# First layer's entry of a hybrid SSD/MLA decoder step: order of squares, weight casts, convolutions and first loads

## Chip, cores and metric

The kernel runs on one core of a Trainium2 chip. The metric is device time in microseconds for one execution; lower is better. The core has a tensor engine (PE, with PEld for its weight loads), a vector engine (DVE), a scalar engine (ACT), GpSimd (POOL) and SyncE (SP, whose queue issues nearly all DMA transfers here).

## The reference

The reference is one inference step of a two-layer decoder in float32: a Mamba-2 SSD layer, then a multi-head latent attention layer, each with an RMSNorm ahead of it and a residual around it. There are 1024 prompt tokens and 8 x 8 sample tokens, 1088 rows of width 1024. Only the first layer's entry matters here:

```python
ln = rms_norm(h, norm_w[0])                       # per token, over 1024
proj = einsum('btd,de->bte', ln, w_in)            # z (2048), xBC (4096), dt (32)
xbc, new_buf = causal_conv(xbc, conv_buf, conv_w, conv_b)   # 4 taps along tokens
xbc = silu(xbc)
dt = softplus(dt_raw + dt_bias);  a_head = -exp(a_log)
y, new_state = ssd_scan(xs, dt, a_head, bm, cm, state)
```

## The kernel before

The whole program is written with a tile framework. The Python code traces instructions in program order; a scheduler with a timeline of its own then lays the order of each engine's queue, and each engine works its queue in that order. A few stages late in the program are ordered by hand; the entry is not.

**Token groups and rows.** The 1088 tokens are cut into three groups `TG` of 384, 384 and 320 columns, and each group into row tiles of 128 tokens (`TILES`, the last of 64). `norm_rows(gi)` loads a group's row tiles `xt` through SP, squares each on ACT with a sum (`sq`, an `ACTIVATE` and a read of the accumulator), takes the reciprocal roots `rs` (a DVE step and a power on POOL, in `rstd_of`), and scales the rows on DVE. There are `XB = 6` row buffers, so the third group's loads wait until the first group's rows have been transposed.

**Columns.** `norm_cols(gi)` turns the scaled rows into columns: for each of the eight blocks `d` of 128 features PE transposes the group's row tiles into one PSUM tile `xtp` (two buffers), ACT writes the rounded high part `xh` with the norm weight as scale (a "single column" below: one `d` of one group), and DVE writes the remainder `xl`. Every float32 product is three products of rounded parts: `xh` by weight high, `xl` by weight high, `xh` by weight low.

**Weights.** `load_w` issues a DMA of raw weights (`wraw`) on SP, splits them into a high part `wih` by a cast on ACT and a low part `wil` by a subtraction on DVE, or on POOL for the third and fourth block of group 0. Each block's weights come in two parts; there are two raw buffers (`RB`) and five pairs of split ones (`WB`).

**Blocks.** `Group` is one of eight SSD head groups. Its four blocks of 128 projected features (B, C and two of x) are projected for the three token groups (`proj_piece`, PSUM tile `pj`, two buffers), copied by ACT into `raw` (two buffers, so the third block needs the first one's), and convolved: ACT makes the first tap into `acc`, and three DVE steps `scalar_tensor_tensor` add the others. For group 0 the first two blocks run interleaved with the norm, token group by token group (`pair(0, both=True)`), and the rest follows after the norm. A SiLU on ACT over both blocks of a pair ends it. `gates` then projects z and, for group 0, dt, with weights split on POOL in `load_zdt` in two halves (`zdh`, `zdl`).

**Order of the entry.** `setup` loads the identity `ident`; `ssd_tiles` loads `alog` and takes its `Exp`; `norm_rows(0)` follows; `before()` loads the small vectors (norm weights, convolution weights) and the first two blocks' weights; `norm_cols(0)`, `norm_rows(1)`; `after()` loads constants and the convolution state; then the first projections, and so on by token group. `norm_rows(gi + 1)` is traced right after `norm_cols(gi)`.

Of the kernel before, what the change touches and what calls it, by code (L numbers as in the profile page):

```python
# [1 line left out]

# [1 line left out]

# [4 lines left out]
F32 = mybir.dt.float32  # L9
# [7 lines left out]
D = 1024  # L17
# [39 lines left out]
PAR = 0.62  # L57
WCOLS = (13, 15, 17, 19)
XDB = 2
YB = 2  # L60
SCAN = "csccsccsccscc"
XB = 6
# [69 lines left out]
def setup(k, stack):  # L132
    tc, nc, I = k.tc, k.nc, k.I
    cp = stack.enter_context(open_pool(tc, name="const", bufs=1))
    k.cp = cp
    k.ident = cp.tile([128, 128], F32, name="ident")
    nc.sync.dma_start(k.ident, I["c_ident"])
    k.nhalf = cp.tile([128, 36], F32, name="nhalf")
    nc.gpsimd.memset(k.nhalf, -0.5)
    k.dram = stack.enter_context(open_pool(tc, name="dram", bufs=1, space=DR))  # L140


def ssd_tiles(k):
    cp, nc = k.cs, k.nc
    k.masku = cp.tile([128, 128], F32, name="masku")
    k.masks = cp.tile([64, 128], F32, name="masks")
    k.negu = cp.tile([128, 128], F32, name="negu")
    k.negs = cp.tile([64, 128], F32, name="negs")
    k.blkm = cp.tile([64, NB], F32, name="blkm")
    k.yssq = cp.tile([128, 9, G], F32, name="yssq")  # L150
    k.tok = cp.tile([128, 9, 4, H], F32, name="tok")
    k.decp = cp.tile([128, H, 8], F32, name="decp")
    k.decs = cp.tile([128, 16, 8], F32, name="decs")
    k.dtb = cp.tile([128, H], F32, name="dtb")
    k.dsk = cp.tile([128, H], F32, name="dsk")
    k.tok3 = cp.tile([96, 2, H], F32, name="tok3")
    k.blk3 = cp.tile([96, 4], F32, name="blk3")
    k.alog = cp.tile([128, H], F32, name="alog")
    nc.sync.dma_start(k.alog, k.I["ssd_a_log"][0].partition_broadcast(128))
    nc.scalar.activation(k.alog, k.alog, AF.Exp)  # L160


def ssd_consts(k):
    nc, I = k.nc, k.I
    nc.sync.dma_start(k.masku, I["c_masku"])
    nc.sync.dma_start(k.masks, I["c_masks"])
    for neg, mask in ((k.negu, k.masku), (k.negs, k.masks)):
        nc.gpsimd.tensor_scalar(neg, mask, -NEG, NEG, op0=ALU.mult, op1=ALU.add)
    nc.sync.dma_start(k.blkm, I["c_blkm"])
    for j in range(3):  # L170
        nc.sync.dma_start(k.blk3[32 * j : 32 * j + 32], I["c_blkm"][:32, :4])
    nc.gpsimd.memset(k.yssq, 1.0)
    nc.sync.dma_start(k.dtb, I["ssd_dt_bias"][0].partition_broadcast(128))
    nc.sync.dma_start(k.dsk, I["ssd_d"][0].partition_broadcast(128))


def load_vectors(k, vp, psum):
    nc, I, cp = k.nc, k.I, k.cp
    if True:
        r1 = vp.tile([128, 128], F32, name="r1")  # L180
        nc.sync.dma_start(r1, I["ssd_conv_w"].rearrange("o k (b c) -> (o k b) c", c=128))
        r2 = vp.tile([68, 128], F32, name="r2")
        nc.sync.dma_start(r2[0:16], I["norm_w"].rearrange("l (b c) -> (l b) c", c=128))
        nc.sync.dma_start(r2[16:48], I["ssd_conv_b"].rearrange("o (b c) -> (o b) c", c=128))
        nc.sync.dma_start(r2[48:64], I["ssd_norm_w"].rearrange("o (b c) -> (o b) c", c=128))
        nc.sync.dma_start(r2[64:68], I["mla_q_norm_w"].rearrange("o (b c) -> (o b) c", c=128))
        k.vec = cp.tile([128, 196], F32, name="vec")
        p = psum.tile([128, 512], F32, tag="tr", name="vecp", bufs=PB["tr"])
        nc.tensor.transpose(p[:, :128], r1, k.ident)
        nc.tensor.transpose(p[:, 128:196], r2, k.ident[:68, :68])  # L190
        nc.vector.tensor_copy(k.vec, p[:, :196])
    k.convw = [k.vec[:, 32 * j : 32 * j + 32] for j in range(4)]
    k.normc = [k.vec[:, 128:136], k.vec[:, 136:144]]
    k.convb = k.vec[:, 144:176]
    k.ssdn = k.vec[:, 176:192]
    k.qn = k.vec[:, 192:196]


def rstd_of(k, out, ssq, n):
    nc = k.nc  # L200
    nc.vector.tensor_scalar(out, ssq, 1.0 / n, EPS, op0=ALU.mult, op1=ALU.add)
    m, n = out.shape[0], int(np.prod(out.shape[1:]))
    e = k.nhalf[:m, :n]
    if len(out.shape) == 3:
        e = e.rearrange("p (a b) -> p a b", a=out.shape[1])
    nc.gpsimd.tensor_tensor(out, out, e, op=ALU.pow)
# [9 lines left out]
def norm_rows(k, gi, load, pool, xbufs):  # L216
    nc = k.nc
    t0, n = TG[gi]
    idx = [i for i, (a, m) in enumerate(TILES) if t0 <= a < t0 + n]
    xs = []  # L220
    ssq = k.cp.tile([128, 3], F32, tag="nssq", name=f"ssq{gi}", bufs=2)
    nc.gpsimd.memset(ssq, 1.0)
    for j, i in enumerate(idx):
        m = TILES[i][1]
        xt = pool.tile([128, D], F32, tag="xt", name=f"xt{i}", bufs=xbufs)
        load(xt, i)
        sq = k.sqp(f"sq{i}")
        nc.scalar.activation(sq[:m], xt[:m], AF.Square, accum_out=ssq[:m, j : j + 1])
        xs.append((xt, m, TILES[i][0] - t0))
    rs = k.cp.tile([128, 3], F32, tag="nrs", name=f"rs{gi}", bufs=2)  # L230
    rstd_of(k, rs, ssq, D)
    for j, (xt, m, o) in enumerate(xs):
        nc.vector.tensor_scalar(xt[:m], xt[:m], rs[:m, j : j + 1], None, op0=ALU.mult)
    return xs


def norm_cols(k, gi, xs, wcol, hi, lo, psum):
    nc = k.nc
    t0, n = TG[gi]
    for d in range(8):  # L240
        p = psum.tile([128, 512], F32, tag="tr", name=f"xtp{gi}_{d}", bufs=PB["tr"])
        for xt, m, o in xs:
            nc.tensor.transpose(p[:, o : o + m], xt[:m, d * 128 : d * 128 + 128], k.ident[:m, :m])
        nc.scalar.activation(hi[:, d, t0 : t0 + n], p[:, :n], AF.Copy, scale=wcol[:, d : d + 1])  # L244
        nc.vector.scalar_tensor_tensor(
            lo[:, d, t0 : t0 + n], p[:, :n], wcol[:, d : d + 1], hi[:, d, t0 : t0 + n].bitcast(F32),
            op0=ALU.mult, op1=ALU.subtract)
    if gi == 2:
        nc.gpsimd.tensor_copy(hi[:, :, T:], lo[:, :, SEQ:].bitcast(F32))


def norm_steps(k, load, wcol, hi, lo, pool, psum, steps, xbufs, before=None, after=None, tail=False):
    if tail:
        for i in range(6, 9):
            k.hrows.append(scale_row(k, i, pool))
    rows = k.hrows[:3] if tail else norm_rows(k, 0, load, pool, xbufs)
    if before is not None:
        before()
        wcol = k.normc[0]
    for gi in range(3):  # L260
        norm_cols(k, gi, rows, wcol, hi, lo, psum)
        if gi < 2:
            rows = k.hrows[3 * gi + 3 : 3 * gi + 6] if tail else norm_rows(k, gi + 1, load, pool, xbufs)
        if after is not None and gi == 0:
            after()
        for st in steps:
            next(st)
# [55 lines left out]
def load_zdt(k, pool):  # L323
    nc = k.nc
    w = k.I["ssd_w_in"][0].rearrange("(k p) e -> p k e", p=128)
    k.wzd = []
    k.dtr = pool.tile([128, 9, H], F32, name="dtr")
    nc.gpsimd.memset(k.dtr[64:, 8], 0.0)
    for j in range(2):
        ks = slice(4 * j, 4 * j + 4)  # L330
        hi = pool.tile([128, 4, 288], F32R, name=f"zdh{j}")
        lo = pool.tile([128, 4, 288], F32R, name=f"zdl{j}")
        raw = load_raw(pool, 4, 288, 1)
        nc.sync.dma_start(raw[:, :, 0:256], w[:, ks, 0:256])
        nc.sync.dma_start(raw[:, :, 256:288], w[:, ks, DIN + CONV :])
        nc.gpsimd.tensor_copy(hi, raw)
        nc.gpsimd.tensor_tensor(lo, raw, hi.bitcast(F32), op=ALU.subtract)
        k.wzd += kslices((hi, lo), 4)


# [73 lines left out]
class Group:  # L414
    def __init__(self, k, g, pools):
        self.k, self.g = k, g
        self.wp, self.rp, self.gp, self.psum, ap = pools
        self.ap = ap[g % 2]
        self.raws = {}
        self.pre = {}  # L420
        self.xc = []
        self.ct = self.gp.tile([128, 4, 27], F32, tag="ct", name=f"ct{g}")
        self.z = None

    def pair(self, pi, both=False):
        k, g, nc = self.k, self.g, self.k.nc
# [23 lines left out]
    def block(self, bi, acc):  # L450
        k, g, nc, wp, rp, gp = self.k, self.g, self.k.nc, self.wp, self.rp, self.gp
        blk = (16 + g, 24 + g, 2 * g, 2 * g + 1)[bi]
        ws = self.pre.pop(bi, None) or self.weights(bi)
        raw = rp.tile([128, RAW], F32, tag="raw", name=f"raw{g}{bi}", bufs=2)
        smp = raw[:, 3 + SEQ :].rearrange("p (b w) -> p b w", w=NT + 3)
        nc.gpsimd.memset(raw[:, 0:3], 0.0)
# [16 lines left out]
        nc.scalar.activation(acc, raw[:, 3:], AF.Identity, bias=k.convb[:, blk : blk + 1],  # L473
                             scale=k.convw[3][:, blk : blk + 1])
        for j in range(3):
            nc.vector.scalar_tensor_tensor(acc, raw[:, j : j + n], k.convw[j][:, blk : blk + 1], acc,  # L476
                                           op0=ALU.mult, op1=ALU.add)

    def conv_out(self):
        k, g, nc, gp = self.k, self.g, self.k.nc, self.gp  # L480
# [1493 lines left out]
```

## Time and profile before

| | |
|---|---|
| median of 3 runs | 1986.58 us (1986.08, 1986.58, 1991.92) |
| profiled execution | 1992.53 us |
| its span, first to last instruction | 1990.7 us |
| PE busy | 1907.3 us (96% of the span) |
| DVE, ACT, POOL busy | 1200.6, 1110.7, 826.7 us |
| mean granted PE clock | 0.991 of full speed |
| DMA | 202.12 MB, mean 102 GB/s |

A row of the timeline gives start, duration, engine, source line, operation, out<-in by tile name, shape and count; in brackets stands the idle time of the engine before it and what ended it. `SPq` marks a DMA issue in SP's queue. Matmuls are pipelined, so the interval between two starts says more than a duration. Buffer numbers are left out of the names.

### The profile page before, as it was taken

Reading aid. Unit: us, or ns where it says so; the run is one execution under the profiler, and the core shown is the slowest. Engines: PE = TensorE matmul, PEld = TensorE weight load, DVE = VectorE, ACT = ScalarE, POOL = GpSimd, SP = SyncE. Lnnn points to the kernel's source line nnn. Section 1 sums busy time; section 2 is a strip of 40 time slices with the busy share of each in tenths; the row PEclk is TensorE's granted clock in tenths of the full one; section 3 lists DMA queues with packets and bytes.
Section 4 is the critical chain, followed back from the end, with each engine's and each line's share of the span. In section 5 each row is a group of like instructions: output and inputs, shape, how many; then the busy total and the mean of one; then the engine's idle time right before and its main releaser. Section 6 shows DMA issues by size and latency. Waiting matters only on the chain. (4 is left out here: it accounts for less than half of the span.)

```text
span 1990.7 us, 33385 instructions
## 1 busy us (share of the span) xinstructions
PE 1907.3 (96%) x12001; PEld 1735.5 (87%) x12001; DVE 1200.6 (60%) x2437; ACT 1110.7 (56%) x2535; POOL 826.7 (42%) x1010
## 2 busy tenths in 40 slices
PE   6999999999999999899999999999999999799998
PEld 5899999999999999788787998997888887688887
DVE  4537566656666656765533114566787786766665
ACT  5456767666666676732214224435777777745552
POOL 1327555555655555443003222204333434855541
PEclk9999999999999999999999999999999999999999
DMA  4213323333333332644534242222211213645451
GB/s 152 59 46 95 96 77 100 81 107 86 92 85 93 80 98 68 200 158 170 166 107 140 95 159 83 83 88 64 59 53 43 52 39 98 189 136 144 138 146 38
DMA packets 181228, 202.12 MB, mean 102 GB/s; under 512 B 18844, under 2 KB 147752, under 8 KB 180680
## 3 DMA queue, kind: packets, MB, share of 16 engines
q1 hardware_dynamic: 176008, 180.21, 30.5%
q0 software_dynamic: 4976, 19.66, 3.1%
q8 instruction: 95, 1.56, 0.3%
q14 instruction: 69, 0.57, 0.1%
q10 hardware_dynamic: 80, 0.13, 0.0%
HBM read 146.65 MB, written 53.28 MB: 100 GB/s over the span
## 5 line engine op out<-in xcount | busy, mean ns | idle before, releaser
L87 PE MATMUL pj<-xh,wih 128*128 128x384 f32 (+1 forms) x768 | 256.3, 338 | 9.2 <-ACT raw L460 4.5
L87 PE MATMUL pj<-xl,wih 128*128 128x384 f32 (+1 forms) x768 | 255.4, 333 | 0.0
L87 PE MATMUL pj<-xh,wil 128*128 128x384 f32 (+1 forms) x768 | 254.7, 332 | 0.0
L476 DVE SCALAR_TENSOR_TENSOR acc<-raw,vec,acc 128x1112 f32<-128x1112 f32 x96 | 141.6, 1478 | 25.6 <-ACT acc L473 24.7
L1332 POOL TENSOR_TENSOR tl<-P,th 128x384 fp32r<-128x384 f32 (+1 forms) x96 | 91.6, 955 | 155.6 <-ACT P L1330 113.8
L87 PEld LDWEIGHTS pj<-xh,wih 128*128 128x128 f32 x768 | 145.3, 190 | 11.5 <-ACT xh L244 5.2
L87 PEld LDWEIGHTS pj<-xl,wih 128*128 128x128 f32 x768 | 146.1, 190 | 0.9
L87 PEld LDWEIGHTS pj<-xh,wil 128*128 128x128 f32 x768 | 145.8, 190 | 0.4
L99 PE MATMUL pz<-wih,xh 128*128 128x256 f32 x504 | 142.8, 287 | 1.0 <-ACT z L516 1.0
L99 PE MATMUL pz<-wil,xh 128*128 128x256 f32 (+1 forms) x504 | 140.2, 284 | 0.0
L1329 ACT ACTIVATE th<-st 128x512 fp32r<-128x512 f32 x192 | 94.6, 492 | 70.6 <-PE st L1325 50.2
L579 ACT ACTIVATE M<-M,tok 128x128 f32<-128x128 f32 (+1 forms) x288 | 90.9, 386 | 70.9 <-DVE M L576 70.4
L99 PE MATMUL pz<-wih,xl 128*128 128x256 f32 x448 | 128.3, 286 | 0.0
L1621 POOL TENSOR_TENSOR kvl<-pgr,kvh 128x1024 fp32r<-128x1024 f32 x32 | 77.5, 2423 | 72.2 <-ACT kvh L1620 72.2
L99 PEld LDWEIGHTS pz<-wih,xh 128*128 128x128 f32 x504 | 95.9, 190 | 1.8 <-ACT z L516 1.5
L576 DVE TENSOR_TENSOR M<-M,negu 128x512 f32<-128x512 f32 x64 | 50.3, 786 | 73.2 <-DMA M<-acs_d 71.0
L1330 ACT ACTIVATE P<-st 128x512 f32<-128x512 f32 x192 | 93.5, 487 | 0.0
L99 PEld LDWEIGHTS pz<-wil,xh 128*128 128x128 f32 (+1 forms) x504 | 92.7, 184 | 0.7
L129 DVE TENSOR_TENSOR wil<-wraw,wih 128x512 fp32r<-128x512 f32 x88 | 72.2, 829 | 31.2 <-ACT wih L128 30.2
L1332 DVE TENSOR_TENSOR tl<-P,th 128x512 fp32r<-128x512 f32 x96 | 74.9, 780 | 21.4 <-ACT P L1330 20.9
L562 POOL TENSOR_TENSOR xdd<-xsT,tok 128x256 f32<-128x256 f32 x64 | 51.4, 803 | 81.9 <-ACT xsT L548 81.4
L99 PEld LDWEIGHTS pz<-wih,xl 128*128 128x128 f32 x448 | 85.3, 190 | 0.1
(827 smaller groups left out, 6318.4 us busy)
## 6 DMA issues: line engine op xcount, KB each, us to landing
wraw<-in_ssd_w_in SPq DMA_DIRECT2D x92, 256.0 KB
M<-acs_d SPq DMA_DIRECT2D x64, 256.0 KB
s<-in_state_ssm SPq DMA_DIRECT2D x32, 256.0 KB
y_d<-y SPq DMA_DIRECT2D x64, 128.0 KB
out_s_ssm<-s SPq DMA_DIRECT2D x32, 256.0 KB
wraw<-in_ssd_w_out SPq DMA_DIRECT2D x12, 512.0 KB
q_d<-qt SPq DMA_DIRECT2D x32, 192.0 KB
qp<-q_d SPq DMA_DIRECT2D x8, 768.0 KB
```

The costliest lines, as they stand in the source:

```text
L87: nc.tensor.matmul(out, a, b, start=(i == 0), stop=(i == n - 1))
L99: nc.tensor.matmul(o, a, b, start=(j == 0), stop=(j == len(ops) - 1))
L129: (eng or nc.vector).tensor_tensor(lo, src, hi.bitcast(F32), op=ALU.subtract)
L476: nc.vector.scalar_tensor_tensor(acc, raw[:, j : j + n], k.convw[j][:, blk : blk + 1], acc, op0=ALU.mult, op1=ALU.add)
L562: nc.gpsimd.tensor_tensor(v3(xdd), v3(xsT), hb(2), op=ALU.mult)
L576: nc.vector.tensor_tensor(M[:m, :, :m], M[:m, :, :m], (k.negs if smp else k.negu)[:m, :m].unsqueeze(1).to_broadcast([m, 4, m]), op=ALU.add)
L579: nc.scalar.activation(M[:m, h, :m], M[:m, h, :m], AF.Exp, bias=tk[:, 0, 4 * g + h : 4 * g + h + 1])
L1329: nc.scalar.activation(th[:, :n], ps[:, :n], AF.Exp, scale=SCALE)
L1330: nc.scalar.activation(P[:, :n], ps[:, :n], AF.Exp, scale=SCALE)
L1332: eng.tensor_tensor(tl[:, :n], P[:, :n], th[:, :n].bitcast(F32), op=ALU.subtract)
L1621: nc.gpsimd.tensor_tensor(rl, raw, rh.bitcast(F32), op=ALU.subtract)
```

## The change

Five edits, all in the first layer's entry.

1. *x rows first.* The load of `ident` moves from `setup` into `load_vectors`, and the load and `Exp` of `alog` move from `ssd_tiles` into `ssd_consts`, which is traced after the first group's columns.
2. *Squares behind single columns.* The columns' ACT instructions are kept in `k.cols[gi]`. The square of row tile `j` of group 1 or 2 is queued on ACT behind column `SQ + j` (2, 3, 4) of the group before. `issue_after(ins)` lays an order, without a semaphore, between `ins` and what the block traces on the same engine. In group 0 the root is taken for each row tile by itself.
3. *Third block's weights.* The first weight casts on ACT of block 2 of SSD group 0 are queued behind the last column (7) of token group 0; their DMA and the POOL subtraction get no edge.
4. *First two convolutions.* The DVE steps of block 1 of group 0 are queued behind the last step of block 0.
5. *z/dt low parts.* The subtraction in `load_zdt` is cut into four.

```diff
 def setup(k, stack):
-    nc.sync.dma_start(k.ident, I["c_ident"])
 def ssd_tiles(k):
-    nc.sync.dma_start(k.alog, k.I["ssd_a_log"][0].partition_broadcast(128))
-    nc.scalar.activation(k.alog, k.alog, AF.Exp)
 def ssd_consts(k):
     nc, I = k.nc, k.I
+    nc.sync.dma_start(k.alog, I["ssd_a_log"][0].partition_broadcast(128))
+    nc.scalar.activation(k.alog, k.alog, AF.Exp)
 def load_vectors(k, vp, psum):
+    nc.sync.dma_start(k.ident, I["c_ident"])
@@ norm_rows
+    rs = k.cp.tile([128, 3], F32, tag="nrs", name=f"rs{gi}", bufs=2)
     for j, i in enumerate(idx):
...
-        nc.scalar.activation(sq[:m], xt[:m], AF.Square, accum_out=ssq[:m, j : j + 1])
+        with k.tc.issue_after(k.cols[gi - 1][SQ + j].ins) if gi else nullcontext():
+            nc.scalar.activation(sq[:m], xt[:m], AF.Square, accum_out=ssq[:m, j : j + 1])
         xs.append((xt, m, TILES[i][0] - t0))
-    rs = k.cp.tile([128, 3], F32, tag="nrs", name=f"rs{gi}", bufs=2)
-    rstd_of(k, rs, ssq, D)
+        if gi == 0:
+            rstd_of(k, rs[:, j : j + 1], ssq[:, j : j + 1], D)
+    if gi:
+        rstd_of(k, rs, ssq, D)
@@ norm_cols
-        nc.scalar.activation(hi[:, d, t0 : t0 + n], p[:, :n], AF.Copy, scale=wcol[:, d : d + 1])
+        k.cols[gi].append(
+            nc.scalar.activation(hi[:, d, t0 : t0 + n], p[:, :n], AF.Copy, scale=wcol[:, d : d + 1]))
@@ load_zdt
-        nc.gpsimd.tensor_tensor(lo, raw, hi.bitcast(F32), op=ALU.subtract)
+        for a in range(4):
+            nc.gpsimd.tensor_tensor(lo[:, a], raw[:, a], hi[:, a].bitcast(F32), op=ALU.subtract)
@@ Group.block
-        ws = self.pre.pop(bi, None) or self.weights(bi)
+        first = g == 0 and bi == 2
+        with k.tc.issue_after(k.cols[0][7].ins) if first else nullcontext():
+            ws = self.pre.pop(bi, None) or self.weights(bi)
...
         for j in range(3):
-            nc.vector.scalar_tensor_tensor(acc, raw[:, j : j + n], k.convw[j][:, blk : blk + 1], acc,
-                                           op0=ALU.mult, op1=ALU.add)
+            with k.tc.issue_after(self.conv.ins) if self.conv else nullcontext():
+                last = nc.vector.scalar_tensor_tensor(acc, raw[:, j : j + n], k.convw[j][:, blk : blk + 1], acc,
+                                                      op0=ALU.mult, op1=ALU.add)
+        self.conv = last if g == 0 and bi == 0 else None
```

More of the change, by code (lines that the diff above doesn't have):

```diff
@@ L1 @@
-from contextlib import ExitStack
+from contextlib import ExitStack, nullcontext
 import numpy as np
@@ L59 @@
 XDB = 2
+SQ = 2
 YB = 2
@@ L259, in norm_steps @@
         wcol = k.normc[0]
+    k.cols = [[], [], []]
     for gi in range(3):
@@ L422, in __init__ @@
         self.ct = self.gp.tile([128, 4, 27], F32, tag="ct", name=f"ct{g}")
-        self.z = None
+        self.z = self.conv = None
     def pair(self, pi, both=False):
```

## The prediction

> **What bounds the kernel now.** I read the page's first part, then the tensor engine's waits in the first 120 us, where all the edited code runs, then the timeline of each engine there.
>
> ```profile
> span 1990.7 us, 33385 instructions
> PE 1907.3 (96%) x12001; PEld 1735.5 (87%) x12001; DVE 1200.6 (60%) x2437; ACT 1110.7 (56%) x2535; POOL 826.7 (42%) x1010
> PE pj L87 <- ACT xh L244: 4.4, 2, 2.6
> PE pj L87 <- ACT raw L460: 4.0, 1, 4.0
> ```
>
> The tensor engine (PE) is busy for 96% of the span, so a change off it is worth only the PE idle time that it removes. The two waits that the edits touch (us in total, times, longest) are 4.4 us for `xh` columns and 4.0 us for a `raw` copy. The rows of PE place them (start, duration, idle before):
>
> ```profile
> 12.42 2.02 PE L243 MATMUL xtp<-ident,xt 128*128 128x128 f32 x6 [2.26 <-DVE xt L233]
> 17.02 1.01 PE L87 MATMUL pj<-xh,wih 128*128 128x384 f32 x2 [2.59 <-ACT xh L244]
> 33.59 0.62 PE L87 MATMUL pj<-xh,wih 128*128 128x384 f32 x2 [1.77 <-ACT xh L244]
> 70.12 0.63 PE L87 MATMUL pj<-xh,wih 128*128 128x320 f32 x1 [4.04 <-ACT raw L460]
> 33.59:66.08 32.49, 32.14 (x188) 28.40 (x188) 18.44 (x24) 16.04 (x31) 11.91 (x16) 1.00 0.14 36
> ```
>
> Projection begins at 17.02, stops for 1.77 us ahead of 33.59, and for 4.04 us ahead of 70.12. Between the last two it is full (the last row, of a table by stretches: length, then each engine's busy time, PE's first; 32.14 of 32.49 us). Three gaps, three terms.
>
> **Term 1, the start.** The ACT rows show why `xh` is late:
>
> ```profile
> 0.74 0.39 SPq L137 DMA_DIRECT2D ident<-in_c_ident  x1
> 1.65 1.38 SPq L696 DMA_DIRECT2D xt<-in_x_prompt  x3
> 8.92 1.06 ACT L228 ACTIVATE sq<-xt 128x1024 f32<-128x1024 f32 x1 [0.16 <-DMA xt<-in_x_prompt]
> 10.72 0.86 POOL L206 TENSOR_TENSOR rs<-rs,nhalf 128x3 f32<-128x3 f32 x1 [9.64 <-ACT wih L128]
> 11.61 2.08 DVE L233 TENSOR_SCALAR xt<-xt,rs 128x1024 f32<-128x1024 f32 x3 [0.15 <-POOL ssq L222]
> 13.60 0.62 ACT L128 CAST wih<-wraw 128x512 fp32r<-128x512 f32 x1 [0.29 <-DMA wraw<-in_ssd_w_in]
> 15.35 1.06 ACT L228 ACTIVATE sq<-xt 128x1024 f32<-128x1024 f32 x1 [1.14 <-DMA xt<-in_x_prompt]
> 16.41 1.03 ACT L244 ACTIVATE xh<-xtp,vec 128x384 fp32r<-128x384 f32 x2
> ```
>
> The first six transposes end at 14.44, the four weight casts at 14.22. Then ACT sits until 15.35 on the transfer of the second group's first row tile, squares it, and only at 16.41 writes the first two columns. The change queues that square behind column 2. Columns 0 and 1 then follow the casts at once.
>
> The loads of `ident` and `alog` leave SP's front, so the first x issue can stand where `ident`'s stood (0.74 against 1.65, 0.9 us earlier), and the third square, which waited 0.16 us for its transfer, ends near 9.2 rather than 10.0. The root is taken for each tile, so behind the last square stand one root (0.86) and one scaling (2.08/3 = 0.69) rather than three: the rows are scaled near 11.2, not 13.69. The price is two more roots on POOL, hidden: POOL had waited 9.64 us before its one. These 2.5 us count only as far as the casts let them. Their weights are issued behind the vectors, where `alog`'s issue is gone and `ident`'s is added, so they gain about 0.5 us by the x rows' lead less that issue. Casts end at 13.7, `xh` follows, and PE follows it by 0.61 (17.02 - 16.41): start at 14.3, gain **2.7 us**. Upper end: `xh` goes ahead of the last two casts, gain 4.2. Lower end: below nothing, by the moved `Exp` (a rival). I take 2.7, because the casts are already ahead of the columns in this row order.
>
> **Term 2, between groups 0 and 1.** The same mechanism:
>
> ```profile
> 31.16 1.06 ACT L228 ACTIVATE sq<-xt 128x1024 f32<-128x1024 f32 x1 [2.92 <-DMA xt<-in_x_prompt]
> 32.12 0.19 ACT L228 ACTIVATION_READ_ACCUMULATOR sq<-xt 128x1 f32 x1
> 37.63 2.06 DVE L233 TENSOR_SCALAR xt<-xt,rs 128x1024 f32<-128x1024 f32 x3
> 37.83 0.58 ACT L244 ACTIVATE xh<-xtp,vec 128x384 fp32r<-128x384 f32 x1 [0.82 <-PE xtp L243]
> 43.81 0.58 PE L243 MATMUL xtp<-ident,xt 128*128 128x128 f32 x3
> ```
>
> ACT waits 2.92 us for the third group's rows, and the copies and columns that PE needs stand behind the square. Queued behind column 2 of group 1, it lets them pass. PE still needs two copies and a column after its last matmul, so I keep 0.4 us of the 1.77: gain 1.4 us.
>
> Part comes back. The three squares (1.06 each and 0.19 for the accumulator) now lie between columns 2 and 5 of group 1, so ACT does 0.58 + 1.25 = 1.83 us per column there. Counting in the old times, column 4 began at 37.83; with three squares in front of the scaling its last square ends about 37.83 + 0.58 + 2.3 x 1.25 = 41.3 (two squares and part of a third come between columns and delay them), and root and scalings (0.86 + 2.06 and short steps) about 44.5. Before they ended at 39.7; the first transposes of group 2 run by 43.81. That costs 0 to 1 us, depending on what PE has queued ahead. I take 0.6: **net 0.8 us**. In group 0 the same queueing is covered by its length: eight columns take the 14.8 us from 17.02, so columns 2 to 4 with their squares fill two thirds of it, about 9.9, and root and scalings (0.86 + 2.08) fit in the 4.9 left.
>
> **Term 3, the convolutions.**
>
> ```profile
> 58.84 1.38 DVE L476 SCALAR_TENSOR_TENSOR acc<-raw,vec,acc 128x1112 f32<-128x1112 f32 x1 [3.26 <-ACT acc L473]
> 61.43 2.40 DVE L476 SCALAR_TENSOR_TENSOR acc<-raw,vec,acc 128x1112 f32<-128x1112 f32 x1
> 62.62 3.74 POOL L337 TENSOR_TENSOR zdl<-wraw,zdh 128x1152 fp32r<-128x1152 f32 x1
> 63.76 3.15 DVE L129 TENSOR_TENSOR wil<-wraw,wih 128x512 fp32r<-128x512 f32 x1
> 68.11 1.36 DVE L476 SCALAR_TENSOR_TENSOR acc<-raw,vec,acc 128x1112 f32<-128x1112 f32 x1
> 69.58 0.86 ACT L460 COPY raw<-pj 128x384 f32<-128x384 f32 x2 [8.55 <-DVE acc L476]
> 71.76 1.91 ACT L437 ACTIVATE acc<-acc 128x2048 f32<-128x2048 f32 x1
> 73.22 0.35 PE L87 MATMUL pj<-xh,wil 128*128 128x320 f32 x1
> ...
> 75.02 0.31 PE L87 MATMUL pj<-xh,wil 128*128 128x320 f32 x1
> ```
>
> The third block's copies start when the fifth of six convolution steps has ended (68.11 + 1.36 = 69.47), so the two blocks' steps are interleaved and the first `raw` buffer is held almost to the end. In a row, block 0's third step is the third on DVE and ends at 63.83; the copies are done by 64.7. PE reaches the point at 66.08 in this frame. The 4.04 us go, with 1.4 us to spare. Behind the gap eleven matmuls of 320 columns take 3.10 us (70.12 to 73.22); the next twelve take 1.80 (73.22 to 75.02), 0.15 each. That slow stretch follows the idle time, and goes with it: 3.10 - 11 x 0.15 = 1.45, together 5.5 us. The 1.77 us of term 2 had no such stretch behind it. Block 1's buffer is freed no later, by the same sixth step.
>
> The `wil` of 3.15 us ends 0.55 after the POOL subtraction (66.36): these two do not run side by side. Cut in four, each piece (a quarter of 2.53, the 3.74 less the 1.21 until the step of 61.43 ended) lets DVE in between. It can delay a step by 0.6, twice of which lies inside the 1.4 us of cover; the added starts fall on POOL, off PE's path. What is late next is the SiLU of the pair (71.76), which waits for the sixth step (68.11 + 2 x 1.36 = 70.8) and can have block 2's last copies behind it on ACT. PE asks for those 24 matmuls of 0.15 and 24 of 384 columns (0.18) after 66.08, at 74.0. SiLU's 1.91 ends at 72.7, at 74.0 with the table load of 1.28 that is quoted below, and a cast, a second SiLU and the copies follow: 0 to 1.5 us. I take 0.5. **Net 5.0 us.**
>
> **Terms at nothing.** The third block's first cast waited 2.49 us on ACT, with `xh` behind it, but PE had other matmuls:
>
> ```profile
> 22.47 0.62 ACT L128 CAST wih<-wraw 128x512 fp32r<-128x512 f32 x1 [2.49 <-DMA wraw<-in_ssd_w_in]
> 17.02:31.82 14.80, 14.75 (x80) 13.54 (x80) 8.11 (x14) 6.95 (x13) 3.09 (x6) 1.00 0.55 164
> ```
>
> PE is busy 14.75 of 14.80 us there: no gain. Queued behind column 7, the cast frees its staging buffer later, and the next weight load, which SP issues into that buffer, moves too. If SP has the third group's rows behind that load they land later as well, but their squares now wait for column 2 of group 1 anyway; that column stands two ahead of the one of 37.83, so some 4 us behind 31.16. I take 0.
>
> The profile's first table load stands ahead of `alog`'s `Exp` at the start. With a `Square` first and the `Exp` later there may be one load more:
>
> ```profile
> 0.73 1.28 ACT L160 ACT_TABLE_LOAD   x1 [0.73 <-PEq L1961]
> ```
>
> That is 1.28 us of ACT, in a stage where ACT is busy 6.95 of 14.80: zero on the path, 1.28 if it falls ahead of `xh`. The Trainium skill ("ScalarE: Activation LUTs", What ACT_TABLE_LOAD costs) says a switch to another set costs about 2.66 us with its drain, and so speaks against moving the `Exp`. By it the sum would lose another 1.4 us where the switch is uncovered; the profile's row shows 1.28 and no drain beside it.
>
> **Sum.** 2.7 + 0.8 + 5.0 = 8.5 us. The profiled execution took 1992.53 us, 1.83 around its span of 1990.7; it would become 1984.0. The runs' median is 1986.58, 5.95 lower than the profiled one. The three gaps belong to the order of the queues, so the same 8.5 us are taken off it: **1978**. With the terms' ends (4.2 or 0; 1.4 or 0.4; 5.5 or 4.0) the case spans 4 to 11 us, 1975.5 to 1982.5; its middle is 1975.5 to 1981. What this kernel's measurement can tell from no change is 0.3%, 6 us.
>
> **Rivals.**
> *The Exp takes the square's place.* `alog` is now loaded behind the second group's rows, and its `Exp` is not tied to a column. The nearest load behind those rows:
>
> ```profile
> 18.14 0.29 POOL L168 TENSOR_SCALAR negu<-masku 128x128 f32<-128x128 f32 x1 [6.52 <-DMA masku<-in_c_masku]
> ```
>
> POOL, which had nothing else to do, got `masku` at 18.14; `alog` stands one issue ahead of it (about 0.6). If the `Exp` stands ahead of column 0, ACT stalls until about 17.5, and PE starts near 18.3: term 1 becomes -1.3 instead of +2.7. Time 1982. Against it: the code traces the `Exp` after all group 0 columns, and a place behind column 1 costs at most 0.5, since PE then has the 12 matmuls of columns 0 and 1. Term 3 at its lower end with term 1 at half lands in the same place. Chance 0.17.
>
> *The wait moves to the z/dt weights.* PE comes to the gates 8.5 us sooner.
>
> ```profile
> 76.77 2.66 POOL L337 TENSOR_TENSOR zdl<-wraw,zdh 128x1152 fp32r<-128x1152 f32 x1
> 87.30 0.38 PE L99 MATMUL pz<-zdh,xh 128*128 128x288 f32 x1
> ```
>
> The second half was ready at 79.43; the first gate matmul would run at 78.8, and it uses the first half. The load of the second waits only for work that moves up too, so I count nothing; unmoved it costs under 0.6 us: 1978.6, inside the forecast.
>
> *Slower: the scans' queues are drawn anew.* The order of each queue comes from the scheduler's own timeline, and other times at the entry may reorder all seven scan groups behind it.
>
> ```profile
> 130.00:500.00 370.00, 363.25 (x2656) 355.68 (x2654) 241.88 (x400) 247.70 (x612) 213.12 (x319) 1.00 0.33 93
> 500.00:900.00 400.00, 386.73 (x2738) 367.38 (x2738) 257.15 (x429) 253.65 (x629) 213.40 (x305) 1.00 0.37 110
> ```
>
> PE idles 6.75 + 13.27 = 20 us there, some 3 for each of seven groups. Two more for each are 14 us: 1992. From 28.5 us of idle on no gain is left. For it: DVE, ACT and POOL are busy for half to two thirds of these stretches, so that placement matters. Against: the edit changes times by under 10 us and no dependency behind the entry. Chance 0.10; the same lottery the other way, to 1970, 0.08.
>
> *The edges change nothing on the chip*, since something else holds the columns: 1986.6, chance 0.05. The transposes' end at 14.44 speaks against it.
>
> **Numbers.** Forecast 0.60, of which 0.02 falls within 0.3%. Faster: 0.58 + 0.08 + 0.05 of the `Exp` case = 0.71. Same: 0.02 + 0.12 + 0.05 + 0.02 = 0.21. Slower: 0.08. The range 1972 to 1988 leaves out most of the reordering cases, about 0.15.
>
> **What would show it.** Right: PE's first projection near 14.3, with no square between the casts and the first two columns; under 0.6 us of PE idle ahead of group 1's first matmul; no PE wait on the `raw` copy and no slow stretch after it; gates reached near 79. Wrong: ACT waiting on `alog` ahead of a column; PE waiting on DVE's scaled rows of group 2 for over 1 us; the entry shorter by 8 us but PE idle above 28 us in the two scan stretches.

## The result, and the profile after

Thirteen runs of each kernel gave a median of 1979.6 us after (1973.73 to 1988.45) and 1987.5 us before (1983.59 to 1991.95). The ratio is 0.996, with a 95% interval from 0.9947 to 0.9973: 7.9 us faster by the medians, against a forecast of 8.5. The profiled execution after took 1988.45 us, the slowest of its thirteen, so its span is only 4.0 us shorter than that of before. That has to be explained too, and the entry must be read by itself.

From the page of after, and from its rows of PE (start, duration, in brackets the idle time before and what ended it):

```profile
span 1986.7 us, 33396 instructions
PE 1909.0 (96%) x12001; PEld 1738.7 (88%) x12001; DVE 1204.0 (61%) x2439; ACT 1110.3 (56%) x2535; POOL 837.9 (42%) x1018
```

```profile
11.29 0.69 PE L248 MATMUL xtp<-ident,xt 128*128 128x128 f32 x2 [0.57 <-DVE xt L238]
15.98 1.01 PE L88 MATMUL pj<-xh,wih 128*128 128x384 f32 x2 [4.00 <-ACT xh L250]
...
28.05 0.52 PE L325 MATMUL cvp<-ident,cst 96*128 96x96 f32 x4 [0.86 <-DVE xl L251]
...
31.79 0.62 PE L88 MATMUL pj<-xh,wih 128*128 128x384 f32 x2 [0.42 <-ACT xh L250]
...
41.55 0.44 PE L88 MATMUL pj<-xl,wih 128*128 128x384 f32 x1 [0.58 <-DVE xl L251]
...
55.86 0.45 PE L88 MATMUL pj<-xh,wih 128*128 128x384 f32 x1 [0.29 <-ACT raw L473]
...
64.43 0.39 PE L88 MATMUL pj<-xh,wih 128*128 128x320 f32 x1
...
80.14 0.38 PE L100 MATMUL pz<-zdh,xh 128*128 128x288 f32 x1
```

Projection begins at 15.98 (before 17.02). The gap ahead of group 1 is 0.42 instead of 1.77. Block 2's last token group, which had waited 4.04 us at 70.12, follows at 64.43 without any idle time, and its matmuls follow each other at 0.15 us from the second on. The gates begin at 80.14 (before 87.30): 7.16 us gained. But the first wait grew: PE had done its transposes early (the two of 11.29) and then stood for 4.00 us. ACT and SP show why:

```profile
7.80 1.06 ACT L231 ACTIVATE sq<-xt 128x1024 f32<-128x1024 f32 x1 [0.35 <-DMA xt<-in_x_prompt]
...
11.56 0.62 ACT L129 CAST wih<-wraw 128x512 fp32r<-128x512 f32 x1 [0.17 <-DMA wraw<-in_ssd_w_in]
14.83 0.62 ACT L129 CAST wih<-wraw 128x512 fp32r<-128x512 f32 x1 [2.65 <-DMA wraw<-in_ssd_w_in]
15.36 1.05 ACT L250 ACTIVATE xh<-xtp,vec 128x384 fp32r<-128x384 f32 x2
...
18.18 1.05 ACT L231 ACTIVATE sq<-xt 128x1024 f32<-128x1024 f32 x1
...
19.21 0.22 ACT L164 ACTIVATE alog<-alog 128x32 f32<-128x32 f32 x1
```

```profile
5.43 3.85 SPq L285 DMA_DIRECT2D wraw<-in_ssd_w_in  x4
9.33 1.45 SPq L708 DMA_DIRECT2D xt<-in_x_prompt  x3
```

No square stands between the casts and the first two columns any more, and the `Exp` of `alog` slipped in behind the square that follows column 2, for 0.22 us, with no table load. The fourth cast, however, waited 2.65 us for its weights, until 14.83; in before it began at 13.60.

The convolutions, from the rows of DVE, POOL and ACT:

```profile
57.44 2.79 DVE L487 SCALAR_TENSOR_TENSOR acc<-raw,vec,acc 128x1112 f32<-128x1112 f32 x2 [3.26 <-ACT acc L483]
60.15 1.78 DVE L130 TENSOR_TENSOR wil<-wraw,wih 128x512 fp32r<-128x512 f32 x1
61.34 6.78 POOL L345 TENSOR_TENSOR zdl<-wraw,zdh 128x288 fp32r<-128x288 f32 x4
61.85 7.45 DVE L487 SCALAR_TENSOR_TENSOR acc<-raw,vec,acc 128x1112 f32<-128x1112 f32 x4
63.88 1.10 ACT L470 COPY raw<-pj 128x384 f32<-128x384 f32 x2 [4.25 <-DVE acc L487]
66.96 1.28 ACT L445 ACT_TABLE_LOAD   x1
69.33 1.92 ACT L445 ACTIVATE acc<-acc 128x2048 f32<-128x2048 f32 x1 [1.09 <-DVE acc L487]
```

The raw buffer is free after the third step and ACT copies at 63.88 (before 69.58). A `wil` still falls between steps 2 and 3, and the four steps beside the POOL pieces take 1.86 us each (7.45 / 4) rather than 1.38; the cover was just large enough for both.

**Where the profiled pair lost 4 us again.** The timelines of before and then of after have the first `sc` matmul of the second layer 8.09 us apart, and the last store 4.07:

```profile
1306.83 0.22 PE L1286 MATMUL sc<-kTh,qTh 96*128 96x128 f32 x1
...
1986.71 0.48 SPq L1870 DMA_DIRECT2D out_y_sample<-h  x1
```

```profile
1298.74 0.22 PE L1298 MATMUL sc<-kTh,qTh 96*128 96x128 f32 x1
...
1982.64 0.48 SPq L1882 DMA_DIRECT2D out_y_sample<-h  x1
```

Two stretches between them, by the table of stretches for before and then for after (the third number from the end of a row is the granted clock):

```profile
1650.00:1700.00 50.00, 45.72 (x246) 37.24 (x246) 36.05 (x78) 35.83 (x78) 26.93 (x26) 0.97 0.34 97
1700.00:1750.00 50.00, 39.06 (x211) 31.99 (x210) 36.46 (x56) 30.86 (x59) 38.97 (x25) 0.90 0.71 213
```

```profile
1650.00:1700.00 50.00, 45.83 (x224) 37.63 (x223) 34.45 (x70) 31.71 (x71) 28.14 (x26) 0.87 0.38 108
1700.00:1750.00 50.00, 40.37 (x226) 34.45 (x226) 35.19 (x56) 31.01 (x59) 33.72 (x22) 0.86 0.66 208
```

The granted clock was 0.87 against 0.97 in the first stretch and 0.86 against 0.90 in the second. At PE's busy share there that is, as an estimate, up to 0.10 x 45.8 + 0.04 x 40 = 6 us of slower work, and 4.0 us of the 8.1 were gone at the last store. Behind the entry every engine works its queue in the same order in both profiles, so the lead of after can be followed from instruction to instruction: on ACT it is 8.2 us at 1500 of before's time, 7.1 at 1660, 7.2 at 1680, 4.5 at 1720 and 4.1 from 1760 to the end. So 3 of the 4 us went between 1680 and 1760, far from the edits. That the lower clock took them fits its size; no run tests it. Against the same profile of before, the lead of `rows_late` (a variant below) grew from 7.3 at the gates to 12.9 at the end. The whole time of a single pair says little about the entry.

### The profile page after: what moved, and what is told of

The parts are those of the page before. It is cut to its first block, busy times and chain, and to the rows that moved or that the text cites. A ratio compares the mean times of both kernels' runs of the same rounds, so it can differ in the third digit from the quotient of the medians.

```text
span 1986.7 us, 33396 instructions
## 1 busy us (share of the span) xinstructions
PE 1909.0 (96%) x12001; PEld 1738.7 (88%) x12001; DVE 1204.0 (61%) x2439; ACT 1110.3 (56%) x2535; POOL 837.9 (42%) x1018
```

## The experiments

The theory was that three ordering edges close three gaps independently. Three questions were open beside it: whether the moved loads do the work at the start; whether the cut of the z/dt subtraction is only a precaution, and the third block's edge worth nothing, as the prediction had costed them. Every kernel's profile has the same four landmarks of PE, which cut the entry into segments (us):

| kernel | projection starts | group 1 starts | block 2 starts | gates start | start to group 1 | group 1 to block 2 | block 2 to gates |
|---|---|---|---|---|---|---|---|
| before | 17.02 | 33.59 | 57.26 | 87.30 | 16.57 | 23.67 | 30.04 |
| after | 15.98 | 31.79 | 55.86 | 80.14 | 15.81 | 24.07 | 24.28 |
| after_r1 | 14.46 | 32.07 | 56.13 | 80.43 | 17.61 | 24.06 | 24.30 |
| after_r2 | 13.48 | 30.22 | 54.29 | 78.57 | 16.74 | 24.07 | 24.28 |
| sq_free | 15.34 | 31.51 | 55.18 | 79.47 | 16.17 | 23.67 | 24.29 |
| conv_free | 13.73 | 33.01 | 57.08 | 87.63 | 19.28 | 24.07 | 30.55 |
| conv_only | 17.11 | 33.43 | 57.11 | 83.29 | 16.32 | 23.68 | 26.18 |
| rows_late | 14.02 | 31.66 | 55.72 | 80.02 | 17.64 | 24.06 | 24.30 |
| old_loads | 14.76 | 30.19 | 54.25 | 78.55 | 15.43 | 24.06 | 24.30 |
| one_root | 14.15 | 30.02 | 54.10 | 78.39 | 15.87 | 24.08 | 24.29 |
| blk3_free | 13.99 | 33.48 | 57.54 | 81.84 | 19.49 | 24.06 | 24.30 |
| best | 13.12 | 29.50 | 53.57 | 77.85 | 16.38 | 24.07 | 24.28 |
| edges_only | 15.00 | 30.65 | 54.70 | 79.00 | 15.65 | 24.05 | 24.30 |
| edges_best | 15.55 | 30.19 | 54.24 | 78.53 | 14.64 | 24.05 | 24.29 |

The last two columns repeat to 0.03 us wherever the same edits bear on them; what varies from run to run lies ahead of group 1. Part of that is PE's pace: its first matmuls of 384 columns follow each other at 0.32 us, later ones at 0.17 to 0.18, and the change came at 20.9 in after and at 17.7 in after_r1, 4.9 and 3.2 us behind the start. So differences of up to about 1 us in the column from start to group 1 need not come from an edit.

**The convolutions' order without the rest, and the rest without it.** `conv_only` is the kernel before with edit 4 alone; `conv_free` is the kernel after with that edge taken out:

```diff
-            with k.tc.issue_after(self.conv.ins) if self.conv else nullcontext():
+            with nullcontext():
```

> The kernel before with edit 4 alone. Theory A: the PE wait of 4.0 us for the raw copy and the 1.5 us of slow matmuls behind it go, nothing else: projection begins at 17.0, first gate matmul at 81.6 to 82, total 5 to 6 us less than before, ratio 0.997. Rival B (the gain needs the POOL pieces too, since the uncut subtraction delays the third step): over 1 us of the wait stays and the gates come at 83 or later.

> Edit 4 undone alone: the convolution steps of the first two blocks may interleave again; the cut of the z/dt subtraction is kept. Theory A (the interleaving holds the first raw buffer): PE waits about 4 us or, as the four POOL pieces now come between the steps, more, for the raw copy, a slow stretch follows, and the first gate matmul is at 85.5 to 88. Rival B (the cut of the POOL subtraction removes the wait, not the order): the wait stays under 1 us and the gates come at 80 to 81.

`conv_only`: median of 12 runs 1985.93 us against 1991.45 of before beside it, ratio 0.9972 (0.9957 to 0.9987). `conv_free`: 1991.97 in its one run. The segment from block 2 to the gates is 30.04 with neither edit, 30.55 with the cut of `zdl` alone, 26.18 with the order alone (1.61 us of PE wait, as rival B had it), 24.28 with both. The other edits don't touch it: it is 24.29 or 24.30 without the squares' edge (`sq_free`), without edit 3 (`blk3_free`) and without edit 1 (`edges_only`). The rows of `conv_only` (POOL, DVE, ACT, PE) show what the order alone leaves:

```profile
62.59 3.12 POOL L337 TENSOR_TENSOR zdl<-wraw,zdh 128x1152 fp32r<-128x1152 f32 x1
63.10 7.90 DVE L477 SCALAR_TENSOR_TENSOR acc<-raw,vec,acc 128x1112 f32<-128x1112 f32 x4
67.00 0.86 ACT L460 COPY raw<-pj 128x384 f32<-128x384 f32 x2 [6.12 <-DVE acc L477]
67.53 0.41 PE L87 MATMUL pj<-xh,wih 128*128 128x320 f32 x1 [1.61 <-ACT raw L460]
```

The third step starts at 63.10, and ACT copies at 67.00. That is 1.29 us, about the length of one step alone (1.38), after the undivided subtraction has ended at 65.71: the step got next to nothing done beside it. PE waits 1.61 us. With the cut the step gets in between the pieces: in after, the copies come at 63.88, while the pieces run from 61.34 to 68.12. `conv_free` shows the reverse: pieces, but the steps interleaved.

```profile
27.89 0.87 PE L325 MATMUL cvp<-ident,cst 96*128 96x96 f32 x4 [3.63 <-DMA cst<-in_state_conv]
...
69.16 0.64 PE L88 MATMUL pj<-xh,wih 128*128 128x320 f32 x1 [3.27 <-ACT raw L470]
69.60 0.47 PE L88 MATMUL pj<-xl,wih 128*128 128x320 f32 x1
```

A wait of 3.27 us is back, with slow matmuls behind it (0.26 to 0.27 us apart). The granted clock of the slow stretches, by the table of stretches for before and for `conv_free` (third number from the end):

```profile
70.12:73.22 3.10, 3.10 (x12) 3.10 (x13) 0.64 (x1) 3.07 (x3) 0.96 (x3) 0.50 0.66 183
69.16:75.20 6.04, 6.04 (x23) 6.04 (x24) 1.88 (x2) 4.25 (x5) 3.15 (x6) 0.50 0.38 101
```

It was 0.50 for twice as long in `conv_free`, which is why the shorter wait made the longer segment. So the cut is worth 1.9 us (26.18 - 24.28) where the order is set, and brought nothing without it. The Trainium skill ("SBUF — State Buffer", SBUF: two separate sides) says that a DVE operation with two SBUF inputs and a GpSimd one that reads SBUF lock each other out for a whole instruction; the rows of `conv_only` agree (a step of 1.38 us that lasted from 63.10 to near 67.0), and on that reading four shorter locks are what the cut bought. The first row of `conv_free` is a new wait, taken up below.

**The squares' edge.** The kernel after, with the squares' place left to the scheduler:

```diff
-        with k.tc.issue_after(k.cols[gi - 1][SQ + j].ins) if gi else nullcontext():
+        with nullcontext():
```

> Edit 2 undone: the squares of groups 1 and 2 stand wherever the scheduler puts them; the rest of the change is kept. In the order that it now writes, the first two columns of group 0 stand ahead of the square of the next group anyway, and one square stands ahead of the copies and columns of group 1. Theory A (the start is set by the last weight cast, the squares matter only between groups): PE begins projecting near 16.0 as in the changed kernel, waits 1.5 to 2 us for the first column of group 1, and the first gate matmul comes about 1 us later, near 81.2 (changed: 80.1; before: 87.3). Rival B (the squares set the start too): PE begins near 17.0 and the gates near 82.

1980.6 us. With the rows loaded first, the scheduler by itself put two columns ahead of the next group's square; ahead of group 1's columns a square stands and waits, as in before (ACT and PE of `sq_free`):

```profile
14.71 1.05 ACT L250 ACTIVATE xh<-xtp,vec 128x384 fp32r<-128x384 f32 x2
15.65 1.05 ACT L231 ACTIVATE sq<-xt 128x1024 f32<-128x1024 f32 x1
...
29.08 1.06 ACT L231 ACTIVATE sq<-xt 128x1024 f32<-128x1024 f32 x1 [2.62 <-DMA xt<-in_x_prompt]
31.51 0.62 PE L88 MATMUL pj<-xh,wih 128*128 128x384 f32 x2 [0.79 <-ACT xh L250]
```

At the start the edge is thus not needed beside edit 1. Ahead of group 1 PE waits 0.79 us without it, not the 1.5 to 2 expected, and 0.42 with it: 0.37 us. Its price stands in the column from group 1 to block 2: 24.07 with it, 23.67 without, 0.40 us, seen in after as the stop of 0.58 at 41.55. Block 2 starts at 55.18 without the edge and between 54.29 and 56.13 in three profiles with it. Beside the other edits no net gain of this edge is shown.

**Loads and roots.** `old_loads` puts `ident`, `alog` and its `Exp` back to the front; `one_root` takes one root for all three row tiles; `rows_late` traces the constants and the convolution state ahead of group 1's rows:

```diff
--- old_loads
+    nc.sync.dma_start(k.ident, I["c_ident"])                 # setup, and out of load_vectors
+    nc.sync.dma_start(k.alog, ...); nc.scalar.activation(k.alog, k.alog, AF.Exp)   # ssd_tiles, and out of ssd_consts
--- one_root
-        if gi == 0:
-            rstd_of(k, rs[:, j : j + 1], ssq[:, j : j + 1], D)
-    if gi:
-        rstd_of(k, rs, ssq, D)
+    rstd_of(k, rs, ssq, D)
--- rows_late
+        if after is not None and gi == 0:
+            after()
         if gi < 2:
             rows = ... norm_rows(k, gi + 1, load, pool, xbufs)
-        if after is not None and gi == 0:
-            after()
```

> Edit 1 undone alone: ident and alog are loaded first again, and the Exp of alog is at the start. Theory A (what ends last ahead of the first column is the fourth weight cast, and the moved loads bring its issue forward by about half a microsecond): the third square ends about 0.9 us later than in the changed kernel, the fourth cast comes within a microsecond of its 12.6 to 14.8, and the first gate matmul moves by less than 1 us from 80.1. Rival B (the first rows' loads set the start): projection begins 0.9 us later or more, gates at 81 or later.

> The root of group 0 taken once for three row tiles again; all else as changed. Theory A (the casts end last): the rows are scaled 2 us later, near 13, the first column still follows the fourth cast where that is late, and the gates move by less than 0.7 us. Rival B (the rows set the start): projection begins 1.5 to 2 us later than the fourth cast allows.

> The changed kernel with the constants and the convolution state traced ahead of the second group's rows, so that SP issues those rows some 6 us later. Theory A (the fourth weight load is late in the changed kernel because the second group's rows share the DMA engines with it): the fourth cast comes near 12 rather than 14.8 and PE begins projecting near 13; what follows may be worse, because the Exp of alog now stands ahead of the first column and the rows come late for their squares. Rival B (the weight load is late by its own issue on SP): the fourth cast stays near 14.8.

One run each: 1980.7, 1987.11 and 1979.6 us. In the entry none is behind after: gates at 78.55, 78.39 and 80.02, against 78.57 to 80.43 in three profiles of after. The scaled rows do come earlier with edit 1 and a root for each row tile, but PE starts when the fourth cast lets ACT write the columns. That cast began between 12.33 and 14.83 in three profiles of one kernel (after; the third row below is `rows_late`, the first two are after_r1 and after_r2):

```profile
13.30 0.62 ACT L129 CAST wih<-wraw 128x512 fp32r<-128x512 f32 x1 [1.00 <-DMA wraw<-in_ssd_w_in]
```

```profile
12.33 0.62 ACT L129 CAST wih<-wraw 128x512 fp32r<-128x512 f32 x1
```

```profile
12.75 0.62 ACT L129 CAST wih<-wraw 128x512 fp32r<-128x512 f32 x1 [0.16 <-DMA wraw<-in_ssd_w_in]
```

By the packets in the trace, the weights come in 512-byte packets and the rows in 4096-byte ones, in the same DMA queue. In the profile after, the 512-byte packets that started in the microsecond from 11 held 146 KB, and 54, 16 and 3 KB in the next three, while the 4096-byte ones rose from 57 to 254, 340 and 406 KB. In `rows_late` no rows were under way and the weights were complete within the microsecond from 12. In after_r2 they were complete by 12, with rows beside them. So a late tail of the weights trickles beside the rows; why the weights run late in some executions stays open, and `rows_late`'s 12.75 alone, within after's own scatter, doesn't prove that the rows cause it. `rows_late` pays for its order elsewhere: its squares wait 2.39 us for rows at 21.24.

**The third block's edge.** In `blk3_free` it is taken out of the kernel after:

```diff
-        with k.tc.issue_after(k.cols[0][7].ins) if first else nullcontext():
+        with nullcontext():
```

> Edit 3 undone alone: the third block's first cast may stand between the columns of group 0 again. The prediction costs it at nothing, since PE is busy 14.75 of 14.80 us there: gates at 79.5 to 81. Rival: ACT, which now also has the squares between these columns, stalls on the cast's weights for 2 us and PE waits for a column: gates at 82.

1986.07 us in one run. From the rows of ACT and PE:

```profile
23.64 0.62 ACT L129 CAST wih<-wraw 128x512 fp32r<-128x512 f32 x1 [3.76 <-DMA wraw<-in_ssd_w_in]
```

```profile
24.80 0.62 PE L88 MATMUL pj<-xh,wih 128*128 128x384 f32 x2 [2.92 <-ACT xh L250]
```

The cast waits 3.76 us (2.49 in before) and now PE waits 2.92 us behind it, where in before it had work; behind that wait the granted clock is 0.50 from 25.3 to 28.7. The gates come at 81.84, as the rival had it, and start to group 1 is 19.49, the longest of all.

**After again, and versions built from the findings.** `after_r1` and `after_r2` are the kernel after, unchanged. `best` adds two things to it: the split of the second half of the first two blocks' weights is queued behind column 1, so that two casts instead of four stand ahead of the columns, and the convolution state gets a tile of its own, loaded right behind those weights (in after it takes one of the squares' buffers and stands behind the constants in SP's queue). `edges_only` is after without edit 1 and with one root for the three row tiles of group 0 (the last point of edit 2); `edges_best` is `edges_only` with the two additions.

```diff
+        if gi == 0 and d == 1:                    # norm_cols
+            for args in k.halves:                 # second halves of blocks 0 and 1
+                with k.tc.issue_after(k.cols[0][1].ins):
+                    split(k, *args)
-    r = k.sqp("cst")[:96]                         # conv_state_T; four DMAs follow
+    k.cst = r = pool.tile([96, D], F32, name="cst")   # in before(), behind the weights
```

> The changed kernel with two edits more: the splits of the second weight halves of the first two blocks are queued on ACT behind column 1, and the convolution state gets a tile of its own, loaded ahead of the second group's rows, so that it need not wait for a square's buffer. Theory A (the start waits for the last weight load, and a start moved forward is given back where PE waits for the convolution state): projection begins near 12.7, PE has no wait over 0.5 us for the convolution state, block 2 begins near 53.5 rather than 55.9, gates near 77.8, total 2 us less than the changed kernel (ratio to before 0.994 to 0.996). Rival B (the DMA engines are the bound of the entry, so that the rows of the next groups are late by what the start gains): projection begins early, but gates come at 79.5 or later.

> The changed kernel once more, for the scatter of its entry. In the runs so far the fourth weight cast came between 12.6 and 14.8 in kernels whose queues are the same up to that point. Theory A (the share that the DMA engines give to the last weight load varies from run to run): the fourth cast comes below 14, projection begins near 14, the gates near 78.5, ratio to before 0.995 to 0.997. Rival B (the profiled run was typical): fourth cast 14.5 to 15, gates 80.

> The changed kernel a third time, for its profile alone. Theory A: fourth cast below 14, gates near 78.5. Rival B: fourth cast 14.5 to 15, gates 80.

> Edits 2 (the edge alone), 3, 4 and 5, without the moved loads and without the root for each tile. Theory A (what sets the start is the square that stood ahead of the first column, then the last weight cast; moved loads and single roots only shorten a chain that ends earlier): projection begins at 14.5 to 15.0, 2 us before the kernel before, gates at 78.5 to 79.5, total within 1 us of the changed kernel. Rival B (the rows set the start as the prediction had it): scaled rows near 13.7, first column after 14.7, start at 15.5 or later, gates 1 us or more behind the changed kernel's.

> As the last, with the second weight halves split behind column 1 and the convolution state loaded early into a tile of its own. Theory A (casts no longer last, so now the rows set the start): projection begins near 14.6, no earlier than without these two, since the rows are scaled at 13.7; gates near 78.5. With the moved loads and single roots the same two edits gave 13.1 and 77.9, so moved loads and roots are worth about 1 us only once the casts are out of the way.

Ratios to before in their sets: `after_r1` 0.9947 (0.9925 to 0.9968), `edges_only` 0.9932 (0.9908 to 0.9956), `edges_best` 0.9936 (0.9913 to 0.9959); `best`, in another set, 0.9962 (0.9946 to 0.9977). `after_r2` took 1982.61 us. The intervals overlap: none of these is told apart from after, so the 2 us that `best` was expected to gain don't show in the whole time. `edges_only`, with its gates at 79.00, shows no gain from edit 1 and the single roots. The entry's rows do differ. The repeats of after started PE 1.5 and 2.5 us earlier than the first profile of it, but stood for about 2 us at a place where the first had stood for 0.86; first after_r1, then after_r2, then `edges_best` (PE):

```profile
26.87 0.52 PE L325 MATMUL cvp<-ident,cst 96*128 96x96 f32 x4 [2.02 <-DMA cst<-in_state_conv]
```

```profile
26.48 0.52 PE L325 MATMUL cvp<-ident,cst 96*128 96x96 f32 x4 [1.93 <-DMA cst<-in_state_conv]
```

```profile
26.41 0.55 PE L337 MATMUL cvp<-ident,cst 96*128 96x96 f32 x4 [0.42 <-DVE xl L248]
```

PE meets the transposes of the convolution state, whose load is late. The two waits are nearly equal, but not what followed; the granted clock in after_r1 and then in after_r2:

```profile
28.00:31.00 3.00, 3.00 (x14) 2.81 (x13) 0.56 (x1) 0.69 (x2) 0.35 (x2) 0.50 0.90 171
28.00:31.00 3.00, 2.55 (x18) 1.95 (x17) 1.36 (x3) 1.81 (x4) 0.01 (x1) 1.00 0.74 149
```

Behind the wait of 2.02 us PE ran at half clock for 3.4 us, behind the one of 1.93 at full clock. So after_r1's fourth cast came early, as theory A had it, and its gates still at 80.43, where rival B had them. The long segments of `conv_free` and `blk3_free` ahead of group 1 hold such a stretch too, behind waits of 3.63 and 2.92 us.

With a tile of its own the wait on the state's load is gone: at that place `edges_best` waits 0.42 and `best` 1.05 us, both for `xl`. In `best` PE started earliest (13.12), but the rows behind the state's load were late then (a square waited 1.84 us at 17.24); its gates at 77.85 are the earliest of all, 0.7 to 2.6 us ahead of after's. `edges_best` began at 15.55, not near 14.6 as expected, since its last transposes ended at 15.09. With the casts out of the way, early loads and single roots are thus worth 2.4 us at the start, but 0.7 at the gates (77.85 against 78.53), by one profile each.

## Why the prediction came out

The median fell in the range and on the side that was forecast, 1.6 us from the number. Only the third term came out as worked out. In the three profiles of after, term 1 gave 1.04, 2.56 and 3.54 us (forecast 2.7) and term 2 gave 0.36, -1.43 and -0.57 (forecast 0.8); with term 3 that makes 7.16, 6.87 and 8.73 against 8.5. The nearness of the sum is in part luck: what a start gained over the forecast, the stage behind it lost. Nor can whole times tell, since their interval reaches from 0.27 to 0.53%, 5.4 to 10.5 us. All this is set against one profile of before; `conv_only`, whose entry is the same up to group 1, repeats its first two landmarks to 0.2 us. The terms, each against its rows:

- **Term 3, 5.0 net: the mechanism held, the size was 5.76** (30.04 to 24.28, the same in eleven profiles with both edits). The whole 4.04 and the slow stretch went, as worked out. The 0.5 for SiLU was not paid: SiLU ended at 71.25, and the gates came on without a gap. What the working had wrong is the role of the cut: it was costed as a precaution, while without it the 1.4 us of cover are overrun by 1.6 us (`conv_only`, with copies at 67.00 instead of the 63.83 of the working). With the pieces, the third step was allowed two delays of 0.6; counted in before's time (block 2 starts 1.40 later there) the copies came at 65.28, 1.45 late, all of the cover.
- **Term 2, 0.8 net: the gap closed, the gain isn't shown.** The gap went from 1.77 to 0.42, 1.35 against 1.4; the squares' give-back was 0.40 against 0.6. Not foreseen was that PE would stand elsewhere ahead of group 1, 0.86 us at 28.05 and about 2 us there in the repeats. From the first projection to block 2 PE took 40.24 us before, 39.88 in the profile after (0.76 less ahead of group 1, 0.40 more behind it), 41.67 and 40.81 in its repeats, and 39.84 in `sq_free`, without the edge.
- **Term 1, 2.7: 1.04 in the profile after, and 2.56 and 3.54 in its repeats.** The step that failed in the profile after is the end of the casts. It was set 0.5 us ahead of before's, from the order of issue; in the profile after the last weights came 1.2 us later than before's. The transposes were early as worked out (done near 12, not 14.4), so this is not the squares but a transfer. And the step "what is late next" stopped at the squares: the convolution state, not named at all, takes up to 2 us back when PE does start early. The three profiles of after reach the gates 6.9 to 8.7 us before the 87.30 of before, against 8.5 in the forecast; what an earlier start gains, the state's wait and, in after_r1, the half clock behind it take back in part.
- **"The cast at nothing" was right in before's times and wrong after the shift**: 2.92 us of PE wait without edit 3.
- **The edit credited with the start** was partly the wrong one. With loads and roots as before, `edges_only` starts at 15.00 and `sq_free`, without the squares' edge but with early rows, at 15.34; with neither, `conv_only` starts at 17.11. Either way past the square is enough.

The rivals: the `Exp` did not take the square's place (0.22 at 19.21). In `one_root` it did hold ACT until its data came, but behind column 1, and PE had the matmuls of columns 0 and 1 and no wait there, as the prediction had it for that place (ACT):

```profile
17.15 0.23 ACT L164 ACTIVATE alog<-alog 128x32 f32<-128x32 f32 x1 [2.58 <-DMA alog<-in_ssd_a_log]
```

For the table loads, the one at the start moved to the first square (3.97, 1.28 us) and none was added before SiLU's. In `conv_free` the next `ACTIVATE` begins at 70.80, after a load of 1.28 from 69.51, so the drain that the Trainium skill adds ("ScalarE: Activation LUTs", What ACT_TABLE_LOAD costs: 2.66 us in all) does not show; here the measurement decides. (The row of before on which the prediction doubted the drain couldn't tell: behind that load ACT waited 2.88 us for `alog` anyway.) The gates did not wait for z/dt weights. Nor were the scans redrawn; the same two stretches, 7.5 us earlier:

```profile
122.50:492.50 370.00, 362.97 (x2653) 355.78 (x2653) 244.72 (x401) 247.78 (x613) 214.93 (x319) 1.00 0.33 93
492.50:892.50 400.00, 387.49 (x2744) 368.25 (x2744) 257.35 (x429) 253.87 (x629) 215.28 (x307) 1.00 0.37 110
```

PE idles 7.03 + 12.51 = 19.5 us in them, 20.0 before; the queues behind the entry have the same order, engine by engine.

## What to carry to other kernels

Split a stage by landmarks that every variant has: here two of three segments repeated to 0.03 us, and single profiles settled what whole times, scattering by 8 to 15 us in their sets of thirteen, could not. When a stage starts earlier, ask for every transfer and every wait that before's idle time covered, not only for those that the edit touches: the state's load and the third block's cast were both free in before. A long two-input POOL operation beside DVE steps that matter was worth cutting into pieces here, and only together with the order that made those steps matter. And price a wait of PE with the clock behind it, not by its length alone.

## What the hardware showed unexpectedly

The scatter of this kernel, 1973.7 to 1988.5 us, goes with the mean granted clock: of the thirteen runs of after the two at 0.994 have spans of 1972.0 and 1975.7 us, the two at 0.988 spans of 1986.7 and 1984.0; it isn't all of it, since the four at 0.992 lie between 1974.3 and 1982.5. In the one pair of profiles shown to the end, most of the difference fell between 1680 and 1760, where PE is busy for less than its full share and DMA for 66 to 71% from 1700 to 1750.

A short wait of PE can cost more than itself: once the first slow stretch of an entry is over, waits of 1.61, 1.77 and 1.93 us were followed by matmuls at full pace, waits of 2.02, 2.92, 3.27, 3.63 and 4.04 us by 3.4 us at a granted clock of 0.50, and by twice that behind the one of 3.27. At half pace 3.4 us do the work of 1.7.

A change of the entry worth 8 us is half of the scatter of whole times: single pairs drawn from the thirteen runs of each differ by anything from 4.9 us slower (1988.45 against 1983.59) to 18.2 us faster (1973.73 against 1991.95).
